# Layer 0's value projection: two chunks of 512 columns with a PSUM bank per token tile, instead of four chunks of 256

## The chip, the core and the metric

The kernel runs on one core of a Trainium2 chip. The metric is the device time of the whole program in microseconds (us). The engines are named as in the profile: PE is TensorE's matmul side and PEld its weight loads, DVE is VectorE, ACT is ScalarE, POOL is GpSimd, SP is the engine whose queue issues most transfers.

## The reference

Two layers over 256 latent tokens and 256 context tokens, width 2048, in float32. Layer 0 projects all 512 tokens with one matrix of 6144 columns and splits the result:

```
qa, ka, va, ga, ub, gb = split(h @ w_in)      # 1024 columns each
ya = neighbourhood_attention(qa, ka, va, ...)  # 8 heads of 128
yb = s5_bidirectional(ub, ...)                 # drive, scan, readout
y  = concat(ya * silu(ga), gelu_glu(yb) * silu(gb)) @ w_out
```

What is changed is the computation of `va`, the values: 512 tokens x 2048 times 2048 x 1024. Layer 1 (grouped-query attention) and the norms are not touched.

## The kernel before, in words

**Matmuls in three parts.** A float32 product is made from two halves of each operand in the faster float32r type. Activations lie in SBUF as `big_h` and `big_l`, 16 k-tiles of 128 x 512 tokens. Each product of a k-tile is three matmuls: high times high, high times low, low times high.

**The weight stream.** `Stream` (lines 338 to 419) carries all weights in one order in pieces of 1024 columns per partition (512 KB). For each piece, `load` issues a transfer on SP into one of four `raw` buffers, `high` makes the `hi` half on ACT (four buffers), `low` subtracts on DVE into `lo` (three buffers). `get` calls `fill`, which issues halves up to three (`lo`) and four (`hi`) pieces on from the piece it then returns, and transfers as `raw` buffers allow:

```
nh, ns = min(self.i + self.n["hi"], n), min(self.i + self.n["lo"], n)   # hi 4, lo 3
```

**The order.** The program's order of instructions on each engine is written out by the trace of this Python code. Work beside the main line stands in generators (`background`); `pump` (line 456), called between groups of matmuls, steps those whose due time by the built-in cost model (`Clock`, line 54) has come, and `force` steps one until a condition holds. Engines then run their queues in that order and wait on semaphores.

**Around the change.** The phase first forms the 16 gate tiles with `aform` (weights stationary, 512 tokens moving, 24 matmuls per piece). Then come the values, `bform4`, called four times (lines 1355 to 1356): a chunk of 256 columns for four token tiles, two token tiles to a bank of the pool `mm`; the activations are stationary and 256 weight columns move. A chunk is four pieces of four k-tiles; for each piece and token tile 12 matmuls are issued and `pump` is called. In the last piece, after the second and the fourth token tile, `done` (`v_out`, line 1345) evacuates a bank: a copy on ACT into `vv0`, a subtraction on DVE into `vv1`, and two transfers of 256 KB to the DRAM tensors `Vd`. The pool `evv` has two buffers of each. After the values the attention heads start; each reads its 128 columns of `Vd` (line 1398).

Beside the values run: `ada_quad` (matmuls into bank `a`, 16 at a time, with 512 KB pieces `aw` loaded as buffers come free), and the S5 generator `s5`: `drive` (uses the three banks of pool `bb`, named `b`), then the scan on DVE, then 16 copies `sx` on ACT written to `Sd`, the table `pe_t` on ACT, and then the 16 output blocks `outp` (line 974): DVE products `ee`, `et`, `di`, matmuls into `sb` banks and one `b` bank `k1` (line 998), copies `kp`, transfers `tt`, matmuls, and the rest.

Of the kernel before, what the change touches and what calls it, by code (L numbers as in the profile page):

```python
# [23 lines left out]
F32 = mybir.dt.float32  # L24
F32R = mybir.dt.float32r
# [5 lines left out]
P = 128  # L31
D = 2048
T = 256
NT = 512
KT = D // P
# [3 lines left out]
EV_IN = 6144  # L39
# [209 lines left out]
def backbone(ctx: ExitStack, tc: tile.TileContext, A, out):  # L249
    nc = tc.nc  # L250
    clock = Clock()
    V, S, PE = Timed(nc.vector, "dve", clock), Timed(nc.scalar, "act", clock), Timed(nc.tensor, "pe", clock)
    GP, SY = Timed(nc.gpsimd, "gp", clock), Timed(nc.sync, "sp", clock)
# [16 lines left out]
    dr = pool(ctx, name="dr", bufs=1, space=bass.MemoryType.DRAM)  # L270
    ctx.enter_context(tc.manual_schedule())

    def bank():
        return bb.tile([P, 512], F32, name="b")
# [17 lines left out]
    def mbank():  # L292
        return mm.tile([P, 512], F32, name="m")
# [7 lines left out]
    big_h = bigp.tile([P, KT, NT], F32R, name="big_h")  # L301
    big_l = bigp.tile([P, KT, NT], F32R, name="big_l")
# [35 lines left out]
    class Stream:  # L338
# [53 lines left out]
                                l[:, :n].rearrange("p (k n) -> p k n", k=nk))  # L392
            self.ns += 1

        def fill(self):

            n = len(self.jobs)
            nh, ns = min(self.i + self.n["hi"], n), min(self.i + self.n["lo"], n)
            while self.nh < nh or self.ns < ns:
                while self.nl < min(self.ns + self.n["raw"], self.i + self.cap, n):  # L400
                    self.load()
                if self.ns < min(ns, self.nh - 1) or self.nh == n:
                    self.low()
                elif self.nh < min(nh, self.nl):
                    self.high()
                else:
                    self.low()
            self.ahead()
# [6 lines left out]
        def get(self):  # L415

            self.fill()
            self.i += 1
            return self.tl.pop(self.i - 1)

    CAP = 4
    ws = Stream()
    W_IN, W_OUT, W_GLU = A["ev_w_in"], A["ev_w_out"], A["s5_glu_w"]
# [9 lines left out]
    def force(b, done=lambda: False):  # L433

        while b in bg and not done():
            clock.floor = b[1]
            step(b)
        clock.floor = 0.0
# [17 lines left out]
    def pump():  # L456
        ws.ahead()
        more = True
        while more:
            more = False  # L460
            for b in list(bg):
                if b[1] <= clock.now():
                    step(b)
                    more = True
# [53 lines left out]
                          stop=(a == 3 and k == 3), skip_group_check=True)  # L518
            pump()

    def bform4(done):

        ps = [mbank().rearrange("p (t n) -> p t n", t=2) for _ in range(2)]
        for a in range(4):
            wh, wl = ws.get()
            for t in range(4):
                c, o = t * P, ps[t // 2][:, t % 2, :]
                for k in range(4):
                    kk = a * 4 + k
                    PE.matmul(o, big_h[:, kk, c:c + P], wh[:, k, :],  # L530
                              start=(a == 0 and k == 0 and t % 2 == 0), stop=False, skip_group_check=True)
                    PE.matmul(o, big_h[:, kk, c:c + P], wl[:, k, :], start=False, stop=False, skip_group_check=True)
                    PE.matmul(o, big_l[:, kk, c:c + P], wh[:, k, :], start=False, stop=(a == 3 and k == 3),
                              skip_group_check=True)
                if a == 3 and t % 2 == 1:
                    done(t // 2, ps[t // 2])
                pump()


    adw = A["ada_w"]  # L540
# [30 lines left out]
    for m in gates:  # L571
        k0 = 2 * NXB if m < NB_ACC - 8 else 0
        ws.add(W_IN, EV_IN, k0, KT - k0, (5 * 1024 if m < 8 else 2 * 1024) + m * P, P)
    for n in range(4):
        for ko in (0, 1):
            ws.add(W_IN, EV_IN, ko * 8, 8, 2 * 1024 + n * 256, 256)
    for h in range(NAH):
        for s in range(2):
            ws.add(W_IN, EV_IN, 0, KT, s * 1024 + h * P, P)
# [21 lines left out]
    Yd = [dr.tile([P, 512], F32, name=f"Yd{m}") for m in range(8)]  # L601
    Bd = [dr.tile([P, 512], F32, name=f"Bd{m}") for m in range(8)]
    Gd = [dr.tile([P, 512], F32, name=f"Gd{m}") for m in range(8)]
    Vd = [dr.tile([P, 2, 4, 256], F32, name=f"Vd{m}") for m in range(4)]
    Sd = [dr.tile([P, 512], F32, name=f"Sd{m}") for m in range(16)]
    Zd = [dr.tile([P, 512], F32, name=f"Zd{m}") for m in range(NAH)]
    Nd = dr.tile([2, P, D], F32, name="Nd")
# [266 lines left out]
    def s5():  # L874
# [60 lines left out]

        yield from several((drive(bt) for bt in range(16)), 6)


        cp = subpool("s5c")
        V.memset(St[:, 0], 0.0)  # L940
# [124 lines left out]
    s5_have = set()  # L1065
# [6 lines left out]
    with ExitStack() as es:  # L1072
# [133 lines left out]
        for b in range(NB):  # L1206
# [11 lines left out]
            for i in range(NB_ACC if b < NXB else 8):  # L1218
                if i % 4 == 0:
                    w = ws.get()  # L1220
# [106 lines left out]
    s5g = background(s5())  # L1327
    for i, m in enumerate(gates):
# [6 lines left out]
        if m < NB_ACC - 8:  # L1335
            part = nxt
            ps = aform(0, NT, KT - 2 * NXB, 2 * NXB)
            V.tensor_add(part, part, ps)
            ps = part
# [3 lines left out]
        SY.dma_start((Bd + Gd)[m], gt)  # L1343

    def v_out(n):
        def done(i, ps):
            vt = [evv.tile([P, NT], F32R, name=f"vv{x}").rearrange("p (t n) -> p t n", t=2) for x in range(2)]
            act(vt[0], ps)
            V.tensor_sub(vt[1], ps, vt[0])
            for x in range(2):  # L1350
                SY.dma_start(Vd[n][:, x, 2 * i:2 * i + 2], vt[x].bitcast(F32))
        return done

    evv = pool(ph1, name="evv", bufs=2, reuse_waits="tile")
    for n in range(4):
        bform4(v_out(n))
    force(adab)
    force(s5g, lambda: "scan" in s5_have)
    ph1.close()
# [31 lines left out]
    def na_head(h, q, k):  # L1391
        (qh, ql), (kh, kl) = q, k
        bias = load_bias(h)
        gl = att.tile([P, NT], F32, name="gl")
        SY.dma_start(gl, Gd[h])
        vh, vl = (att.tile([P, 4, P], F32R, name="v" + x) for x in "hl")
        for x, t in enumerate((vh, vl)):
            SY.dma_start(t.bitcast(F32), Vd[h // 2][:, x, :, (h % 2) * P:(h % 2) * P + P])
        yield
        V.tensor_add(bias.rearrange("p t (k c) -> p t k c", k=4), bias.rearrange("p t (k c) -> p t k c", k=4),  # L1400
                     negm[:, None, None, :].to_broadcast([P, 2, 4, 64]))
        pl = [bank(), bank()]
        for t in range(2):
            c = T + t * P
            mm3(pl[t], qh[:, c:c + P], ql[:, c:c + P], kh, kl, True, True)
        pc = bank().rearrange("p (t k) -> p t k", t=2)
        for t in range(2):
            mm3(pc[:, t], qh[:, t * P:(t + 1) * P], ql[:, t * P:(t + 1) * P], kh[:, :T], kl[:, :T], True, True)
        scored.add(h)
        yield  # L1410
        pr = att.tile([P, 2, NT], F32, name="pr")
        pr2 = att.tile([P, 2, T], F32, name="pr2")
        mx = att.tile([P, 4], F32, name="mx", bufs=2)
        sm = att.tile([P, 4], F32, name="sm", bufs=2)
        for t in range(2):
            act(pr[:, t, :T], pl[t][:, :T], scale=SCALE)
            V.scalar_tensor_tensor(pr[:, t, T:], pl[t][:, T:], SCALE, bias[:, t], op0=OP.mult, op1=OP.add)
        V.tensor_reduce(mx[:, 0:2], pr, axis=AX.X, op=OP.max)
        V.tensor_reduce(mx[:, 2:4], pc, axis=AX.X, op=OP.max)
        V.tensor_scalar(mx[:, 0:2], mx[:, 0:2], -1.0, None, op0=OP.mult)  # L1420
        V.tensor_scalar(mx[:, 2:4], mx[:, 2:4], -SCALE, None, op0=OP.mult)
        yield
        for t in range(2):
            act(pr[:, t], pr[:, t], AF.Exp, bias=mx[:, t:t + 1], accum_out=sm[:, t:t + 1])
        for t in range(2):
            act(pr2[:, t], pc[:, t], AF.Exp, bias=mx[:, 2 + t:3 + t], scale=SCALE, accum_out=sm[:, 2 + t:3 + t])
        V.reciprocal(sm, sm)
        for t in range(2):
            V.tensor_scalar(pr[:, t], pr[:, t], sm[:, t:t + 1], None, op0=OP.mult)
        for t in range(2):  # L1430
            V.tensor_scalar(pr2[:, t], pr2[:, t], sm[:, 2 + t:3 + t], None, op0=OP.mult)
        yield
        def transposed(src):
            p = bank()
            for k_ in range(2):
                for t in range(2):
                    PE.transpose(p[:, k_ * T + t * P:k_ * T + (t + 1) * P], src(t, k_), ident)
            return softmax_pt(p)

        def value(s_, k0, o, start, stop):  # L1440
            for k_ in range(2):
                mm3(o, vh[:, k0 + k_], vl[:, k0 + k_], s_[0][:, k_], s_[1][:, k_],
                    start and k_ == 0, stop and k_ == 1)

        s_ = transposed(lambda t, k_: pr[:, t, k_ * P:(k_ + 1) * P])
        s2 = transposed(lambda t, k_: pr[:, t, (2 + k_) * P:(3 + k_) * P])
        po = bank()
        yield
        value(s_, 0, po[:, T:], True, False)
        s3 = transposed(lambda t, k_: pr2[:, t, k_ * P:(k_ + 1) * P])  # L1450
        value(s2, 2, po[:, T:], False, True)
        yield
        value(s3, 0, po[:, :T], True, True)
        z = att.tile([P, NT], F32, name="zo")
        V.tensor_mul(z, po, gl)
        if h == NAH - 1:
            zl.append(z)
        else:
            SY.dma_start(Zd[h], z)
        yield  # L1460
# [499 lines left out]
```

## Time and profile before

| | us |
|---|---|
| median of 3 runs | 1521.24 (1519.86 to 1521.37) |
| the profiled execution | 1517.6 |
| its span, first to last instruction | 1515.7 |
| PE busy in the span | 1472.3 (97%) |
| DVE busy | 958.2 (63%) |
| ACT busy | 645.8 (43%) |
| mean granted TensorE clock | 0.989 |

Busy PE time counts pipelined matmuls at their full length, so neighbouring ones overlap; the time that a matmul takes out of PE is its distance to the next. The chain of waits is followed back from the last instruction, at each step to what released it.

### The profile page before, as it was taken

The page shows a single profiled execution, that of the slowest core. Times are in us where ns is not written, and L with a number is a line of the kernel's source. Part 1 is how long each engine was busy: PE and PEld are TensorE (multiplying, and loading weights), DVE is VectorE, ACT ScalarE, POOL GpSimd, SP SyncE. Part 2 cuts the span into 40 slices and gives each one's busy share as a digit, 9 for nine tenths or more (in the row PEclk, how much of TensorE's full clock was granted, in tenths as well). Part 3 has the DMA queues.
Part 4 walks back from the last instruction along what each step waited for, and adds up shares of the span by engine and source line. Part 5 has one row for each costly group of instructions (what it writes and reads, how often), then busy time and mean ns, then how long its engine had stood idle before and what let it go on. Part 6 is the DMA issues. An engine that isn't in the chain of part 4 may idle for free.

```text
span 1515.7 us, 30530 instructions
## 1 busy us (share of the span) xinstructions
PE 1472.3 (97%) x12530; PEld 1281.6 (85%) x12530; DVE 958.2 (63%) x1721; ACT 645.8 (43%) x981; POOL 153.7 (10%) x308
## 2 busy tenths in 40 slices
PE   6999999999999999999999999999999999999995
PEld 3676877777789977888788999999999999999995
DVE  5356468788422888544447765755765766677587
ACT  2333345422455434433345433433454555656540
POOL 1000000000000032300000000100511211121021
PEclk8999999999999999999999999999999999999998
DMA  9999376776897676677776698885566454445684
GB/s 326 337 333 291 111 219 211 227 244 215 264 292 251 176 198 150 162 236 232 216 243 222 234 351 288 272 303 181 173 205 181 128 158 132 140 120 151 211 252 143
DMA packets 329920, 332.70 MB, mean 220 GB/s; under 512 B 40197, under 2 KB 287925, under 8 KB 329141
## 3 DMA queue, kind: packets, MB, share of 16 engines
q1 hardware_dynamic: 323540, 314.87, 66.5%
q0 software_dynamic: 6240, 15.88, 3.9%
q8 instruction: 98, 1.61, 0.4%
q14 instruction: 42, 0.34, 0.1%
HBM read 301.92 MB, written 24.54 MB: 215 GB/s over the span
## 4 chain that ended last, share of the span: by engine, by line
PE 83%; DMA 5%; DVE 4%; issue 4%; POOL 2%; ACT 1%; SPq 1%; DVEq 0%; POOLq 0%; ACTq 0%
PE m L212 61%; PE b L212 12%; PE a L212 6%; PE sb L212 4%; DMA raw<-in_ev_w_in_dram 1%; DVE t L212 1%; SPq L212 1%; DMA aw<-in_ada_w_dram 1%; DMA gf<-in_ln_b_dram 1%; DMA nat<-in_s_c_im_dram 1%; POOL gbr L212 1%; POOL rt L212 1%; DVE lo L212 1%; DMA tt<-kp 0%; POOL xp L212 0%
## 5 line engine op out<-in xcount | busy, mean ns | idle before, releaser
L212 ACT ACTIVATE hi<-raw 128x1024 fp32r<-128x1024 f32 (+1 forms) x253 | 265.2, 1050 | 306.9 <-PE m L212 164.2
L212 PE MATMUL m<-hi,big_h 128*128 128x256 f32 x1224 | 351.3, 287 | 0.2 <-DVE t L212 0.2
L212 PE MATMUL m<-hi,big_l 128*128 128x256 f32 x1224 | 347.1, 284 | 0.0
L212 DVE TENSOR_TENSOR lo<-raw,hi 128x1024 fp32r<-128x1024 f32 (+1 forms) x214 | 257.3, 1209 | 112.5 <-issue 54.5
L212 PE MATMUL m<-lo,big_h 128*128 128x256 f32 x1152 | 326.5, 283 | 0.0
L212 PE MATMUL m<-big_h,hi 128*128 128x512 f32 (+1 forms) x848 | 319.1, 376 | 1.9 <-DVE acc L212 1.2
L212 PE MATMUL m<-big_l,hi 128*128 128x512 f32 (+1 forms) x848 | 309.1, 364 | 0.0
L212 PE MATMUL m<-big_h,lo 128*128 128x512 f32 (+1 forms) x832 | 304.4, 366 | 0.0
L212 PEld LDWEIGHTS m<-hi,big_h 128*128 128x128 f32 x1224 | 235.2, 192 | 7.4 <-issue 6.7
L212 PEld LDWEIGHTS m<-hi,big_l 128*128 128x128 f32 x1224 | 235.3, 192 | 0.2 <-DVE big_l L212 0.2
L212 PEld LDWEIGHTS m<-lo,big_h 128*128 128x128 f32 x1152 | 221.5, 192 | 0.1
L212 PEld LDWEIGHTS m<-big_h,hi 128*128 128x128 f32 x848 | 159.9, 189 | 39.6 <-issue 11.3
L212 PEld LDWEIGHTS m<-big_h,lo 128*128 128x128 f32 x832 | 157.0, 189 | 26.4
L212 PEld LDWEIGHTS m<-big_l,hi 128*128 128x128 f32 x848 | 160.2, 189 | 21.1
L212 PE MATMUL m<-lox,big_h 128*128 128x256 f32 x384 | 108.6, 283 | 0.0
L212 PE MATMUL m<-hix,big_h 128*128 128x256 f32 x312 | 89.1, 285 | 0.0
L212 PE MATMUL m<-hix,big_l 128*128 128x256 f32 x312 | 88.3, 283 | 0.0
L212 POOL DMA_DIRECT2D Yd<-ys x64 | 37.7, 595 | 395.8 <-DVE ys L212 395.1
L212 PEld LDWEIGHTS m<-lox,big_h 128*128 128x128 f32 x384 | 73.6, 192 | 0.3
L212 ACT ACTIVATE hix<-raw 128x1024 fp32r<-128x1024 f32 x45 | 47.5, 1056 | 53.3 <-DMA raw<-in_od_w_out_dram 17.9
L212 PE MATMUL a<-aw,cst 128*32 128x256 f32 x1024 | 64.8, 383 | 1.2 <-DMA aw<-in_ada_w_dram 1.2
L212 DVE TENSOR_TENSOR lox<-raw,hi 128x1024 fp32r<-128x1024 f32 x39 | 47.6, 1222 | 22.3 <-PE m L212 15.7
(383 smaller groups left out, 2167.9 us busy)
## 6 DMA issues: line engine op xcount, KB each, us to landing
aw<-in_ada_w_dram SPq DMA_DIRECT2D x128, 512.0 KB, 5.8
raw<-in_od_w_in_dram SPq DMA_DIRECT2D x96, 512.0 KB, 3.8
raw<-in_ev_w_in_dram SPq DMA_DIRECT2D x90, 512.0 KB, 4.9
adp<-in_ada_w_dram SPq DMA_DIRECT2D x64, 512.0 KB, 7.9
raw<-in_ev_w_out_dram SPq DMA_DIRECT2D x64, 512.0 KB, 5.0
raw<-in_od_w_out_dram SPq DMA_DIRECT2D x32, 512.0 KB, 4.3
ub<-Ud SPq DMA_DIRECT2D x32, 128.0 KB, 4.9
Sd<-sx SPq DMA_DIRECT2D x16, 256.0 KB, 6.1
```

The lines of the kernel that those rows point to most:

```text
L212: r = f(*a, **kw)
```

## The change

The values are formed in two chunks of 512 columns. A chunk has 8 pieces of two k-tiles and 512 columns each (rows of 2 KB in DRAM instead of 1 KB). Four banks are taken per chunk, one for each token tile: both of `mm` and two of the three of `bb`; before the first chunk the S5 generator is stepped until its `drive` part is through. Pieces are taken in pairs (`get2`). For each pair and token tile, 12 matmuls of 512 columns are issued in two parts of 6, each followed by `pump`. In the last pair `done` follows each token tile. `Vd` becomes two tensors. Matmuls of this part: 768 of 256 columns before, 384 of 512 after.

```diff
-        def fill(self):
+        def fill(self, m=99):
-            nh, ns = min(self.i + self.n["hi"], n), min(self.i + self.n["lo"], n)
+            nh, ns = min(self.i + min(m, self.n["hi"]), n), min(self.i + min(m, self.n["lo"]), n)
...
+        def get2(self, fill=True):
+            if fill or self.ns < min(self.i + 2, len(self.jobs)):
+                self.fill()
+            self.i += 2
+            return self.tl.pop(self.i - 2), self.tl.pop(self.i - 1)
...
-    def bform4(done):
...
+    def wpart(ps, w, c, korder, a):
+        wh, wl = w
+        for k in range(2):
+            kk = korder[a * 2 + k]
+            PE.matmul(ps, big_h[:, kk, c:c + P], wh[:, k, :], start=a == 0 and k == 0, stop=False)
+            PE.matmul(ps, big_h[:, kk, c:c + P], wl[:, k, :], start=False, stop=False)
+            PE.matmul(ps, big_l[:, kk, c:c + P], wh[:, k, :], start=False, stop=a == 7 and k == 1)
+        pump()
+
+    def wide4(done, korder, ps):
+        for a in range(4):
+            w = ws.get2(a < 3)
+            for t in range(4):
+                for j in range(2):
+                    wpart(ps[t], w[j], t * P, korder, 2 * a + j)
+                if a == 3:
+                    done(t, ps[t])
+                    if t == 0:
+                        ws.fill(1)
...
-    for n in range(4):
-        for ko in (0, 1):
-            ws.add(W_IN, EV_IN, ko * 8, 8, 2 * 1024 + n * 256, 256)
+    for n in range(2):
+        ws.add(W_IN, EV_IN, 0, KT, 2 * 1024 + n * 512, 512)
...
-    Vd = [dr.tile([P, 2, 4, 256], F32, name=f"Vd{m}") for m in range(4)]
+    Vd = [dr.tile([P, 2, 4, 512], F32, name=f"Vd{m}") for m in range(2)]
...
         yield from several((drive(bt) for bt in range(16)), 6)
+        s5_have.add("drive")
...
-        def done(i, ps):
-            vt = [evv.tile([P, NT], F32R, name=f"vv{x}").rearrange("p (t n) -> p t n", t=2) for x in range(2)]
+        def done(t, ps):
+            vt = [evv.tile([P, 512], F32R, name=f"vv{x}") for x in range(2)]
             act(vt[0], ps)
             V.tensor_sub(vt[1], ps, vt[0])
             for x in range(2):
-                SY.dma_start(Vd[n][:, x, 2 * i:2 * i + 2], vt[x].bitcast(F32))
+                SY.dma_start(Vd[n][:, x, t], vt[x].bitcast(F32))
...
-    for n in range(4):
-        bform4(v_out(n))
+    force(s5g, lambda: "drive" in s5_have)
+    for n in range(2):
+        wide4(v_out(n), tuple(range(KT)), [mbank(), mbank(), bank(), bank()])
...
-            SY.dma_start(t.bitcast(F32), Vd[h // 2][:, x, :, (h % 2) * P:(h % 2) * P + P])
+            SY.dma_start(t.bitcast(F32), Vd[h // 4][:, x, :, (h % 4) * P:(h % 4) * P + P])
```

## Rows read from the trace of the kernel before

**Rows 1.** The page's chain of waits: shares of the span by line.
```profile
PE m L212 61%; PE b L212 12%; PE a L212 6%; PE sb L212 4%; DMA raw<-in_ev_w_in_dram 1%; DVE t L212 1%; SPq L212 1%; DMA aw<-in_ada_w_dram 1%; DMA gf<-in_ln_b_dram 1%; DMA nat<-in_s_c_im_dram 1%; POOL gbr L212 1%; POOL rt L212 1%; DVE lo L212 1%; DMA tt<-kp 0%; POOL xp L212 0%
```

**Rows 2.** Busy time by stretch: from:to, length, PE, PEld, DVE, ACT, POOL, clock, DMA.
```profile
412.00:441.00 29.00, 29.00 (x267) 26.05 (x266) 6.22 (x7) 15.07 (x20) 0.00 (x0) 1.00 0.88 284
495.00:528.00 33.00, 32.14 (x569) 30.25 (x569) 27.68 (x46) 13.78 (x28) 2.39 (x4) 1.00 0.56 163
```

**Rows 3.** Instructions on tile m, 395 to 545: count, duration min/median/max, first and last start.
```profile
L212 PE MATMUL m<-hi,big_h x256: 278/283/386, 412.4 to 527.4; 128*128 128x256 f32 x128
```

**Rows 4.** Chain of waits in order of time, 412 to 500: start, length, what.
```profile
460.94 5.94 PE m L212 x48
466.88 1.00 PE a L212 x16
467.88 8.82 PE m L212 x72
```

**Rows 5.** The same chain, 300 to 400, in the gates.
```profile
309.37 5.71 PE m L212 x24
...
316.07 7.75 PE m L212 x33
```

**Rows 6.** The same chain, 500 to 545, between S5's output blocks.
```profile
509.76 0.50 PE sb L212 x24
...
511.89 4.50 PE m L212 x36
...
517.00 1.62 PE m L212 x12
...
533.16 1.59 PE m L212 x6
```

**Rows 7.** Timeline of DVE: start, length, instruction, idle before and releaser.
```profile
440.97 0.69 DVE L212 TENSOR_TENSOR vv<-m,vv 128x512 fp32r<-128x512 f32 x1 [3.37 <-ACT vv L212]
...
473.80 1.23 DVE L212 TENSOR_TENSOR lo<-raw,hi 128x1024 fp32r<-128x1024 f32 x1 [4.43 <-issue]
...
506.38 1.21 DVE L212 TENSOR_TENSOR lo<-raw,hi 128x1024 fp32r<-128x1024 f32 x1
...
509.64 1.21 DVE L212 TENSOR_TENSOR lo<-raw,hi 128x1024 fp32r<-128x1024 f32 x1
```

**Rows 8.** Timeline of SP's queue, 435.5 to 443.
```profile
436.90 1.05 SPq L212 DMA_DIRECT2D Vd<-vv  x2
```

**Rows 9.** Timeline of ACT, 434 to 519.
```profile
436.28 0.60 ACT L212 ACTIVATE vv<-m 128x512 fp32r<-128x512 f32 x1 [1.82 <-PE m L212]
...
505.45 1.06 ACT L212 ACTIVATE hi<-raw 128x1024 fp32r<-128x1024 f32 x1 [3.47 <-PE m L212]
507.86 0.27 ACT L212 ACTIVATE kp<-b 128x112 f32<-128x112 f32 x1 [1.35 <-PE b L212]
```

**Rows 10.** Transfers on tile Vd, 430 to 470, first two chunks: issue to landing.
```profile
DMA to landing us min/median/max: 5.9/6.5/7.3
```

**Rows 11.** Transfers on tile Vd, 485 to 540, last two chunks: issue to landing.
```profile
DMA to landing us min/median/max: 2.4/2.4/2.4
```

**Rows 12.** Who waited for whom on PE, 500 to 530: total, times, longest.
```profile
PE sb L212 <- DVE di L212: 0.9, 1, 0.9
```

**Rows 13.** Instructions on tile dT: the matmuls of drive, first and last start.
```profile
L212 PE MATMUL b<-ub,dT x512: 222/222/369, 212.6 to 299.2; 128*64 128x64 f32 x171
```

**Rows 14.** Timeline of PE, 506 to 511 and 574 to 586.
```profile
510.19 0.30 PE L212 MATMUL b<-ee,bbar 64*32 64x112 f32 x4
...
580.43 1.34 PE L212 MATMUL sb<-sx,ee 128*64 128x64 f32 x32 [3.55 <-DMA sx<-Sd]
```

**Rows 15.** DMA issues, 425 to 432: count, KB each, median us to landing.
```profile
aw<-in_ada_w_dram SPq DMA_DIRECT2D x3, 512.0 KB, 6.7
```

**Rows 16.** DMA queues, 440 to 450: packets, MB, share of 16 engines.
```profile
q1 hardware_dynamic: 1565, 3.16, 97.2%
```

**Rows 17.** Busy time by stretch, columns as in rows 2.
```profile
580.00:585.00 5.00, 4.57 (x42) 3.88 (x43) 3.91 (x7) 0.89 (x3) 2.35 (x4) 0.66 0.91 204
```

## Prediction before the run

> **What bounds the kernel now.** I read the chain of waits first: it is to be seen there that matmuls of TensorE (PE) into four kinds of banks carry 61 + 12 + 6 + 4 = 83% of the span, those into the `m` banks most, and no single kind of transfer over 1% [rows 1]. So a change counts by the PE time that it takes out or puts in. Then the stretches of the values' stage: PE is busy 29.00 of 29.00 us in its first quarter and 32.14 of 33 in its last; VectorE (DVE) has 6 us of work in the first and 28 in the last, where the S5 output blocks run [rows 2]. Then the groups by shape: the stage's 768 matmuls are three groups of 256, each 128x256, from 412.4 us on (one of the three stands there) [rows 3]. Their 283 ns are the length of one in the pipeline, not its share of the time; the distance from one to the next comes from the chain, where only the number of matmuls differs between two steps: (8.82 - 5.94) / 24 = 0.120 us [rows 4].
>
> **The matmuls.** 768 of 256 columns go, 384 of 512 come; the stationary operand is the same 128x128 token block, so half as many weight loads go with them. The stage of before has no 512-wide matmul; the gates ahead of it have, with split weights and `big_h`/`big_l` in exchanged roles: (7.75 - 5.71) / 9 = 0.2267 us from one to the next [rows 5]. 768 x 0.120 = 92.2 us against 384 x 0.2267 = 87.1: -5.1 us. From the other side: 512 columns at twice 0.120 would save nothing. I take the row, since width and clock (1.00, which is 2.4 GHz) are the same and only the source of the moving columns differs.
> Against the columns alone at that clock (107 and 213 ns) both distances are 13 ns longer: a fixed part per matmul, and 384 times it is the 5.1 us.
> The Trainium skill (TensorE: Matmul & The Clock Gate, section Back-to-back issue gap) gives the isolated gap as N/2.4 + 2.5 ns, so a fixed part of only 2.5, and by it the exchange would be worth 83.9 - 82.9 = 1.0 us; the rows, at 13, disagree with it.
>
> **Entering and leaving.** A run of value matmuls between two other groups takes more than its count: 48 take 5.94 us, 0.18 over 48 x 0.120 [rows 4]; 24 wide ones 5.71, 0.27 over 24 x 0.2267 [rows 5]. Ten ada groups of 16 lie inside the stage (one row of the ten stands there [rows 4]) and stay, so 10 x 0.09 = 0.9 us comes back. Around S5's blocks it is 1.62 for 12 (0.18 over) against 1.59 for 6 (0.23 over) [rows 6]; some eight such edges give 0.4. Together +1.3 us. Bounds: 0.4 (the ada edges alike after all) and 2.
>
> **The split of the weights.** Now two pieces are used per step. There are three `lo` buffers, and `get2` leaves pieces split up to one beyond the pair, so at each call the second piece of the coming pair has no `lo` yet. Its buffer is that of the last pair's first piece, which PE reads until six matmuls (1.36 us) before the pair ends. The subtraction takes 1.21 to 1.23 us [rows 7], and PE asks for its result seven matmuls (1.59 us) after the pair's start. Where DVE has nothing else, 1.36 + 1.59 covers 1.23 and it costs nothing; this holds for five of the seven steps from one pair to the next. Before, each `lo` was made two pieces (11.5 us) ahead. `get2(False)` in the last pair does not hold back: seven pieces are split where eight are wanted, so it fills as always, and `fill(1)` then finds nothing to do but loads.
>
> **The step from the first chunk to the second.** Here the cover is gone. The four evacuations now follow each other at 12 matmuls, 2.72 us, where before two stood 2.9 us apart and then 24 us passed. Each takes one `vv0` and one `vv1` of which there are two, so the third and fourth evacuation wait for the `Vd` transfers of the first and second. With S the start of the chunk's last pair: the second token tile ends at S + 5.44; its activation starts 0.2 later and takes 0.6, its first transfer is issued at S + 6.25 (436.90 for an activation at 436.28) [rows 8, 9], the other 0.8 later after the subtraction. In this stretch a `Vd` transfer lands 5.9 to 7.3 us after issue, median 6.5 [rows 10]: so S + 13.55 until both buffers are free, then the fourth subtraction (0.69) [rows 7] and behind it on DVE the `lo` of the second piece (1.23): S + 15.5. PE wants it at S + 10.88 + 1.59 = S + 12.5. A wait of 3.0 us; in general landing time less 3.5. Behind the waiting activation on ScalarE (ACT) stand the next pair's two `hi` (2.1 us, wanted 10.9 us later) and S5's `sx` copies, behind DVE's wait only the two `lo`. Bounds: 1.2 us where the transfers land at 2.4 as in the late evacuations [rows 11], since the subtraction and the `lo` still come one after the other; 3.8 at 7.3. I take 3.0, the median of this stretch. At the second chunk's end the transfers land at 2.4 us and the buffers are free in time: nothing.
>
> **The last pair.** At its start S5's blocks fill DVE. In the trace PE releases ACT's `hi` of that boundary at 505.45 [rows 9], but its `lo` runs at 509.64, 4.2 us late, behind S5's work and behind the `lo` of the boundary before it, which ran at 506.38 [rows 7]. One of these two falls away: 3.0 us late, done 4.2 after the boundary. PE wants it at 1.6 plus the S5 block that stands in between, 2.1 us (509.76 to 511.89) [rows 6]. That is 0.5 us. Bounds: -0.9, if the wait of 0.9 us for `di` [rows 12] goes with the earlier start; +2.9, if none of the lag is taken up and no block stands in between (5.4 - 1.6 = 3.8, less the 0.9).
>
> **At nothing.** The two banks from S5's pool: `drive` ended at 299.2 us [rows 13], so the `force` runs nothing. For the second chunk S5's output blocks have one bank for `k1` instead of three; the copy out of it starts at 507.86 and takes 0.27, the next block writes at 510.19 [rows 9, 14], 2 us to spare; without that cover some 0.6 us a block, four blocks. `Vd` keeps its 16 writes of 256 KB, the weights 16 loads of 512 KB on SP, in longer rows; the reads per head keep 512-byte rows. The ada pieces land 6.7 us after issue [rows 15], and groups come every 5.94 + 1.00 us now, 6.71 then: PE did not wait for them [rows 2], so nothing; if it were tight all through, 10 x 0.23 = 2.3 us are lost.
>
> **Sum.** -5.1 + 1.3 + 3.0 + 0.5 = -0.3 us: a span of 1515.4 and an execution of 1517.3 against the profiled 1517.6 (1515.7 and 1.9 around it). That execution is 3.6 us below the median of the runs; on the median, 1521.24 - 0.3 = 1520.9 us. What remains after the stage is bound by PE again, so a gain or loss there carries to the end.
>
> **Rivals.** About 0.2%, 3.0 us, is what a measurement tells from no change.
> Faster: the waits stay at their lower bounds, since the transfers land early and DVE is ahead of PE in the last pair. Then -5.1 + 1.3 + 1.2 - 0.9 = -3.5: 1517.7 us. For it: DVE idles through most of the first three quarters, and late transfers land at 2.4 us [rows 11]. Against: the third and fourth evacuation fall into the loaded stretch.
> Slower: the boundary wait grows until the clock falls. Eight `Vd` transfers (2.1 MB) now come within 9 us on queues that are at 97.2% of their share with four [rows 16]. A PE wait of 3.55 us in this trace (up to 580.43) was followed by a granted clock of 0.66, between its two levels of 1.2 and 2.4 GHz, over 5 us [rows 14, 17]: 1.7 us lost. At a landing time of 9 us the wait is 5.5, with the clock 7.2 instead of 3.0: 1520.9 + 4.2 = 1525.1 us. It decides the sign from a landing time of 8.1 us on (4.6 + 1.7 = 6.3, a sum of +3.0). Against: the first two evacuations, whose landing counts, are no denser than before.
> No saving in the matmuls: if 512 columns from the weight buffers take twice what 256 take (0.240), the sum is 1.3 + 3.0 + 0.5 = +4.8 and the time 1526.0 us. The rows of the gates speak against it [rows 5].
> By the skill's formula above the sum would be +3.8 and the time 1525.0; it goes with this rival's chance.
>
> **How the numbers follow.** Forecast 0.43, faster rival 0.28, slower rival 0.22, no saving 0.07. With the boundary wait between 1.2 and 3.8 us and the last pair's between -0.9 and 1.5 the forecast's own range is 1518 to 1523; the range goes on to the rivals, 1516.6 to 1525.8. Faster by over 0.2% (below 1518.2): most of the faster rival and the low edge of the forecast, 0.27; slower (above 1524.3): the last two and a little of the forecast, 0.28; within: 0.45.
>
> **What would show it.** The distance of the wide value matmuls (0.227). One gap on PE of 2 to 4 us, six to seven matmuls into the second chunk, put down to `lo` on DVE, and the third and fourth `vv` activation waiting for `Vd`. A wait of 0 to 2 us in the last pair. The ada groups entered and left 0.09 us dearer. It is wrong if PE shows no gap at the boundary, or if the wide distance is 0.24.

## The result, and the profile after

The changed kernel takes 1530.47 us (median, 1523.52 to 1537.86) against 1519.47 for the kernel before (1516.66 to 1521.37): ratio 1.0063 with a 95% interval of [1.0048, 1.0078]. The medians are 11.0 us apart, and the new one lies outside the predicted range of 1516.6 to 1525.8. The profiled execution took 1529.65 us, its span is 1527.9 at a clock of 0.987.

The loss is read best by cutting both spans at the same instructions. Ahead of the values every engine has the same instructions in the same order, so the time of any of them can be compared. The row is that of the drive inputs written to `Ud`; the last two numbers are the starts of the first and last issue. Before, then after:

```profile
L212 SPq DMA_DIRECT2D Ud<-up x8: 319/328/348, 187.8 to 194.1; - x8
```
```profile
L212 SPq DMA_DIRECT2D Ud<-up x8: 319/328/350, 194.2 to 200.5; - x8
```

6.4 us are lost before anything that was changed has run. What PE waited for in the second half of that time, from 90 us to 188 in before and to 194 in after (total us, times, longest):

```profile
PE m L212 <- DVE acc L212: 1.2, 1, 1.2
PE sb L212 <- DMA nat<-in_s_c_im_dram: 0.9, 1, 0.9
```
```profile
PE sb L212 <- DMA nat<-in_s_c_im_dram: 2.2, 1, 2.2
PE sb L212 <- DMA nat<-in_s_b_im_dram: 1.8, 1, 1.8
PE m L212 <- DVE acc L212: 1.4, 1, 1.4
```

`nat` is the buffer into which S5's weights `s_b_re`, `s_b_im`, `s_c_re` and `s_c_im` are loaded, 512 KB each. PE waited 4.0 us for two of these loads, against 0.9 before, and behind these waits the clock cost 3.4 us (it was at 1.2 GHz for 3.4 us from 99.3 and again from 157.3), against nothing before. The 3.1 us more of waiting and the 3.4 of clock are the early loss.

The first value matmul comes at 412.4 before [rows 3] and at 419.0 after. The second cut is the last pair of splits of the attention output in layer 0, on DVE, before and after:

```profile
861.00 1.29 DVE L212 SCALAR_TENSOR_TENSOR big_l<-za,big_h 128x512 fp32r<-128x512 f32 x2
```
```profile
870.42 1.29 DVE L212 SCALAR_TENSOR_TENSOR big_l<-za,big_h 128x512 fp32r<-128x512 f32 x2
```

From the first value matmul to this cut, "the middle" below, it is 448.6 us before and 451.4 after; from there to the end, "the rest", 654.7 and 657.4. So the 12.2 us between the two spans are, to within rounding, 6.6 early, 2.8 in the middle, 2.7 in the rest. What the change was priced for lies in the middle alone.

Who waited on PE there (total us, times, longest), 412 to 861 before, then 419 to 870 after:

```profile
PE sb L212 <- DMA sx<-Sd: 3.6, 1, 3.6
PE sb L212 <- DVE di L212: 0.9, 1, 0.9
PE a L212 <- ACT aw L212: 0.7, 1, 0.7
```
```profile
PE m L212 <- DVE lo L212: 3.8, 2, 2.3
PE sb L212 <- DMA tt<-kp: 2.8, 3, 2.0
PE sb L212 <- DVE di L212: 2.3, 1, 2.3
PE a L212 <- DMA aw<-in_ada_w_dram: 0.9, 1, 0.9
```

5.2 us of waits have become 10. The two for `lo`, 3.8 us, are the predicted ones; those for S5 (`tt`, `di`, `sx`) changed places, 4.5 before and 5.1 after. The chain of waits in order of time shows the wide matmuls and the step between the chunks (start, length, what):

```profile
437.77 1.00 PE a L212 x16
438.77 1.60 PE m L212 x6
440.38 4.10 PE b L212 x18
444.48 1.00 PE a L212 x16
...
467.86 7.33 DMA Vd<-vv
476.54 1.23 DVE lo L212
477.81 5.74 PE m L212 x17
```

24 wide matmuls between two ada groups take 1.60 + 4.10, 5.71 us from 438.77 to 444.48, to the hundredth what 24 took in the gates [rows 5]. The stretches of [rows 2] again, 6.6 us later (columns as there):

```profile
419.00:448.00 29.00, 28.06 (x166) 20.14 (x165) 6.55 (x6) 14.84 (x18) 0.00 (x0) 1.00 0.79 252
502.00:535.00 33.00, 29.21 (x466) 22.76 (x465) 25.81 (x43) 14.73 (x27) 2.40 (x4) 1.00 0.57 156
```

PE falls from 32.14 to 29.21 us in the second. In the rest, waits for ada weights (before at 950 to 1060, after at 957 to 1070):

```profile
PE a L212 <- DMA aw<-in_ada_w_dram: 0.9, 1, 0.9
```
```profile
PE a L212 <- DMA aw<-in_ada_w_dram: 3.0, 1, 3.0
```

### The profile page after: what moved, and what is told of

Its sections match the earlier page's. It is cut to its first block, busy times and chain, and to the rows that moved or that the text cites. A ratio compares the mean times of both kernels' runs of the same rounds, so it can differ in the third digit from the quotient of the medians.

```text
span 1527.9 us, 29770 instructions
## 1 busy us (share of the span) xinstructions
PE 1473.9 (96%) x12146; PEld 1262.3 (83%) x12146; DVE 958.4 (63%) x1721; ACT 645.1 (42%) x981; POOL 154.1 (10%) x308
## 4 chain that ended last, share of the span: by engine, by line
PE 80%; DMA 7%; DVE 4%; issue 4%; POOL 2%; ACT 1%; SPq 1%; DVEq 0%; ACTq 0%; POOLq 0%
PE m L212 58%; PE b L212 13%; PE a L212 6%; PE sb L212 4%; DMA raw<-in_ev_w_in_dram 2%; DMA aw<-in_ada_w_dram 1%; DVE t L212 1%; DMA nat<-in_s_b_im_dram 1%; DMA nat<-in_s_c_im_dram 1%; DMA gf<-in_ln_b_dram 1%; SPq L212 1%; POOL gbr L212 1%; DMA tt<-kp 1%; POOL rt L212 1%; DVE lo L212 1%
## 5 line engine op out<-in xcount | busy, mean ns | idle before, releaser
L212 PE MATMUL m<-hi,big_h 128*128 128x256 f32 (+1 forms) x1032 | 304.5, 295 | 0.7 <-DVE t L212 0.7
L212 PE MATMUL m<-hi,big_l 128*128 128x256 f32 (+1 forms) x1032 | 300.8, 292 | 0.0
L212 PE MATMUL m<-lo,big_h 128*128 128x256 f32 (+1 forms) x960 | 280.3, 292 | 3.8 <-DVE lo L212 3.8
L212 PEld LDWEIGHTS m<-hi,big_h 128*128 128x128 f32 x1032 | 199.2, 193 | 7.8 <-issue 4.7
L212 PEld LDWEIGHTS m<-hi,big_l 128*128 128x128 f32 x1032 | 199.0, 193 | 3.0 <-DVE big_l L212 0.2
L212 PEld LDWEIGHTS m<-lo,big_h 128*128 128x128 f32 x960 | 185.4, 193 | 7.0 <-DVE lo L212 4.5
L212 PEld LDWEIGHTS m<-hix,big_h 128*128 128x128 f32 x312 | 59.8, 192 | 0.9 <-issue 0.4
```

What stands on the lines that cost most here:

```text
L212: r = f(*a, **kw)
```

## The experiments

The table has, of each profile, the start of the first `Ud` issue, the middle with PE's idle time and the time lost to the lower clock in it (half of the time at 1.2 GHz), and the rest (of the padded kernels without the padding). The median stands beside that of before on the same chip; e7 and e8 are one execution each.

| kernel | Ud | middle | idle | clock | rest | median / before |
|---|---|---|---|---|---|---|
| before | 187.8 | 448.6 | 5.2 | 1.7 | 654.7 | 1519.47 |
| after | 194.2 | 451.4 | 10.2 | 1.7 | 657.4 | 1530.47 / 1519.47 |
| e1 before again | 187.4 | 448.5 | 5.0 | 1.7 | 652.7 | 1520.9 / 1520.82 |
| e2 after again | 193.0 | 454.4 | 11.0 | 5.1 | 656.7 | 1531.0 / 1520.82 |
| e3 after, ring of 4 | 190.2 | 454.0 | 9.6 | 6.8 | 657.7 | 1526.87 / 1520.82 |
| e4 before, new Vd | 187.9 | 448.4 | 4.9 | 1.7 | 654.6 | 1520.86 / 1520.82 |
| e5 single, ring of 4 | 192.4 | 460.2 | 12.0 | 6.8 | 657.6 | 1530.8 / 1521.62 |
| e6 single, ring of 2 | 187.9 | 457.4 | 11.5 | 8.5 | 657.9 | 1532.6 / 1521.62 |
| e7 after, padded | 188.1 | 455.6 | 10.4 | 6.8 | 657.2 | 1538.68 / 1521.62 |
| e8 before, padded | 188.6 | 450.5 | 5.9 | 3.4 | 655.2 | 1532.84 / 1521.62 |
| e9 e6, ada 1.0 us apart | 194.5 | 445.3 | 5.5 | 0.0 | 657.8 | 1523.37 / 1521.37 |
| e10 before, ada 1.0 us apart | 190.8 | 448.3 | 4.3 | 1.7 | 659.3 | 1519.95 / 1521.37 |
| e11 as e7 | 192.3 | 453.8 | 8.4 | 6.8 | 661.1 | 1538.71 / 1521.37 |
| e12 as e8 | 187.9 | 449.5 | 5.6 | 1.7 | 655.5 | 1531.42 / 1521.37 |
| e13 before, S5 loads in 1 KB | 190.1 | 448.6 | 5.1 | 1.7 | 655.6 | 1521.01 / 1522.22 |
| e14 after, S5 loads in 1 KB | 190.1 | 451.7 | 8.6 | 3.4 | 657.9 | 1527.48 / 1522.22 |
| e15 before, S5 loads on POOL | 188.3 | 445.7 | 3.0 | 0.0 | 658.5 | 1524.85 / 1522.22 |
| e16 after, S5 loads on POOL | 188.4 | 457.4 | 14.0 | 6.8 | 658.0 | 1535.57 / 1522.22 |
| e17 e9, ada matmuls later | 193.3 | 448.8 | 6.5 | 3.4 | 653.9 | 1521.29 / 1522.78 |
| e18 e10, ada matmuls later | 187.9 | 448.9 | 5.3 | 1.7 | 653.5 | 1521.83 / 1522.78 |

**e1 and e2, both kernels again.**

> The kernel before, once more, for a second profile. In the first one the values' stage began at 412.4 us; in the changed kernel's it began at 419.0, although the program's order of instructions on every engine is the same up to there. Theory A (the first 412 us differ from one execution to the next): this run may begin its values anywhere from 411 to 420 us, and the time is within 0.2% of before (ratio 0.998 to 1.002). Theory B (the early part depends on the kernel, by where its DRAM tensors lie): the values begin at 412 to 413 us again.

> The changed kernel once more. Theory A: its values may begin anywhere from 411 to 420 us; the stage and what follows it together are again 5 to 6 us longer than before, ratio 1.003 to 1.006. Theory B: the values begin at 418 us or later, ratio 1.005 to 1.008. Both: a wait of PE of 1.2 to 4 us for lo near the start of the second chunk.

Before: ratio 0.9998 [0.9982, 1.0013]. After: 1.0065 [1.005, 1.0079]. The loss is there again, the early 5 to 6 us among it: the values begin at 411.9 and at 418.2 us. That is theory B's forecast, but later profiles don't keep to it: the changed values begin at 411.9 and 413.4 in e6 and e7, the old ones at 415.6 in e10.

**e3, evacuation buffers 4 deep.**

```diff
-    evv = pool(ph1, name="evv", bufs=2, reuse_waits="tile")
+    evv = pool(ph1, name="evv", bufs=4, reuse_waits="tile")
```

> The changed kernel with four buffers of vv0 and vv1 instead of two, so that no evacuation waits for a Vd transfer. If that ring is what delays the split at the step from the first chunk to the second: PE's wait for lo there falls from 2.3 us to 1.2 or less, the drop of the clock behind it (0.94 over 468 to 495 us) goes, S5's table pe_t comes some 3 us earlier after the start of the values, and the run is 3 to 6 us faster than the changed kernel. If instead the pairs as such (one lo too few) cost the time, the wait stays above 2 us and the time within 2 us of the changed kernel.

1.0037 [1.0023, 1.005]. Waits on PE in its middle:

```profile
PE sb L212 <- DVE di L212: 4.9, 1, 4.9
PE sb L212 <- DMA tt<-kp: 3.8, 5, 1.5
PE a L212 <- ACT aw L212: 0.7, 1, 0.7
```

No wait for `lo` is left: with the pairs, a ring of two makes them, as predicted. But 4.9 us of waiting turn up at S5's first output block instead, the clock costs 6.8 us in place of 5.1, and the middle is as long as in e2. The median is 4.1 us under e2's, as forecast, but not for the reason forecast: in the profile 2.8 us of the gain stand at the early mark.

**e4, before with the changed `Vd` alone** (two tensors of 512 columns).

> The kernel before with only its DRAM tensors for the values laid out as in the changed kernel (two of 512 columns instead of four of 256; the order of the work is the same). Theory A: no change, ratio 0.998 to 1.002. Theory B: slower by 4 to 7 us, with the loss before 200 us.

1.0008 [0.9996, 1.0021], nothing early and nothing in the middle: the tensor's layout alone does not cost the time.

**e5 and e6, one piece at a time.**

```diff
-        for a in range(4):
-            w = ws.get2(a < 3)
+        for a in range(8):
+            w = ws.get()
             for t in range(4):
-                for j in range(2):
-                    wpart(ps[t], w[j], t * P, korder, 2 * a + j)
-                if a == 3:
+                wpart(ps[t], w, t * P, korder, a)
+                if a == 7:
                     done(t, ps[t])
-                    if t == 0:
-                        ws.fill(1)
```

> After, but the 512-column weights are split and used one piece at a time (eight pieces a chunk, as before) and evacuation buffers are 4 deep. In the two profiles of after, the stretch from the first value matmul to the end of layer 0 (the last split of the attention output) is 451.4 and 454.4 us long against 448.6 before, and PE sits idle in it for 10.2 and 11.0 us against 5.2. Theory A (the pairs and the short ring make the weights late): no wait for lo in 410-560, idle back to 5 to 6 us, that stretch 443 to 446 us, the median 1521 to 1524 us with the early loss still there. Theory C (S5's output blocks are paced by VectorE, and shorter matmuls cover less of it): the lo waits go, PE waits for di and tt instead, idle stays at 9 to 11 us, the stretch 451 to 454 us, the median 1526 to 1530 us. Early loss (Ud issued at 190 to 194 against 187.8): either size, A and C say nothing of it.

> After with one piece at a time and evacuation buffers still 2 deep, so that the pairs alone are undone. Theory A: the ring alone keeps one lo wait of 2 to 3 us at the chunk boundary, idle 7 to 8 us, the stretch from the first value matmul to the end of layer 0 446 to 449 us, median 1523 to 1526 us. Theory C: as after, idle 9 to 11 us, 451 to 454 us, median 1527 to 1531 us.

1.006 [1.0036, 1.0084] and 1.008 [1.0052, 1.0108]: both medians and both middles lie above what either theory gave, theory A's by far. The waits fit neither. In e6's middle they are

```profile
PE a L212 <- DMA aw<-in_ada_w_dram: 6.9, 8, 4.1
PE sb L212 <- DMA tt<-kp: 2.1, 4, 0.9
PE sb L212 <- DVE di L212: 1.8, 2, 1.1
PE a L212 <- ACT aw L212: 0.7, 1, 0.7
```

No `lo` even with two buffers, and less for S5 than before had. All of the added idle time is a new wait, some 250 us behind the values, for ada weights: S5 finishes later by the planner's clock, the ada loads beside the heads start a head later, and their last two groups are forced together ahead of the last head (e5 has 4.1 us of it, in seven waits). The stretch has the clock at 0.66 of its full 2.4 GHz on the mean:

```profile
775.00:800.00 25.00, 17.38 (x139) 8.87 (x132) 6.38 (x15) 5.17 (x7) 0.00 (x0) 0.66 0.70 231
```

**e9 and e10, that pile taken away; and before with the same number.**

```diff
-            adab = background(ada_quad(1, 1, 1024, ap3, 8, 8, 2.0))
+            adab = background(ada_quad(1, 1, 1024, ap3, 8, 8, 1.0))
```

> e6 (one piece at a time, evacuation buffers 2 deep) with one number changed: the 32 loads of ada weights that run beside the heads of layer 0 are asked for 1.0 us apart instead of 2.0. In e6 PE waited 6.7 us for aw at 778 to 793 and its clock was at 1.2 GHz for 17.1 us there (8.5 us lost), because the last two groups of ada matmuls were left over for the last head. Theory D (what e5 and e6 lost is this pile alone; the values in single pieces are a gain): waits for aw under 1.5 us, no fall of the clock at 780 to 800, the stretch from the first value matmul to the end of layer 0 442 to 445 us against 457.4 in e6 and 448.6 in before, the median 1513 to 1519 us by where the early part falls. Theory C (S5's blocks cost the time in any layout): the pile goes, and 4 us and more come back as waits for di and tt: 448 to 452 us, median 1520 to 1525 us.

> Control for e9: before with the same one number (ada loads 1.0 us apart). Before has no such pile (one wait of 0.72 us for aw at 786), so the median stays at 1520 to 1522 us; if it falls by over 2 us, the gain of e9 is not the values'.

e9: 1.0009 [0.9989, 1.0028]; e10: 0.9993 [0.9978, 1.0009]. The same stretch of e9 has PE at 23.54 us and the clock at 1.00:

```profile
775.00:800.00 25.00, 23.54 (x166) 18.35 (x165) 14.60 (x26) 12.35 (x22) 0.00 (x0) 1.00 0.80 242
```

The pile is gone, as theory D has it, and the middle is 445.3, 3.3 under before and just above D's 442 to 445. PE's waits for S5's blocks are 3.7 us against 4.5 in before, so C's waits did not come. But the median, 1523.37, misses D's 1513 to 1519 and lies in C's range: by the time alone nothing is gained, since this profile lost 6 us early and 3 in the rest. Of theory A this is left: the waits for `lo` need both the pairs and the ring of two, for e3, with a deeper ring, and e6, without the pairs, have none. What the pairs cost with the two numbers of e9 and e17 was not run.

**e17 and e18, the wait in the rest; and before with the same two numbers.**

```diff
-            clock.ready = when[n0 + g - 1] + 1.0
+            clock.ready = when[n0 + g - 1] + (3.0 if (l, s) == (1, 2) else 1.0)
```

> e9 with a second number changed: the ada matmuls beside layer 0's output projection are put 3.0 us behind the planned landing of their weights, not 1.0. In e9 one of them held PE for 2.88 us at 991.7 and the clock was at 1.2 GHz for 3.4 us behind it (1.7 us lost). If that wait is what the late part costs: no wait for aw over 0.9 us at 950 to 1060, the stretch from the end of layer 0 to the end 653 to 655 us against 657.8 in e9 and 652.7 to 654.7 in before, the median 2 to 5 us under e9's, 1516 to 1521 us, 0.1 to 0.4 per cent under before. If the late part has another cause, it stays at 657 to 658 us and the median at e9's 1.001 of before.

> Control: before with the same two numbers. Before waits for aw 0.88 us at 988, so there is at most 1 us to gain: 1518 to 1521 us. What e17 has under this is the values'.

e17: 0.999 [0.9972, 1.0008], e18: 0.9996 [0.9976, 1.0016]. All waits on PE of e17 at 950 to 1065:

```profile
PE b L212 <- DVE t L212: 0.3, 1, 0.3
```

The wait for `aw` is gone and the rest is 653.9 against 657.8 in e9, as forecast: that wait, and the clock behind it, made e9's late loss. The wait isn't the values' own: in e10, before with one number changed, the planner puts the group early as well, PE waits 1.8 us for it, and the rest is 659.3, which the wait explains only in part. e17 takes back the 10 us of after, but its median, 1521.29, just misses the forecast of 1516 to 1521, and it isn't told from before, nor from e18. Its middle is 448.8, as long as e18's 448.9 and 3.5 us longer than e9's; one wait for `aw` is 1.2 longer there (1.95 us at 789.3) and the clock takes 3.4. So the shorter middle stands in one profile of two.

**e7, e8, e11, e12, the early loss: padding at the end.** 384 tiny matmuls behind the last one that counts give after as many matmuls as before has.

```diff
                 SY.dma_start(dram(out, i * P * D + c * 512, [[D, P], [1, 512]]), parts[c][0])
+        pad = mbank()[:32, :32]
+        for i in range(384):
+            PE.matmul(pad, ident[:, :32], ident[:, :32], start=True, stop=True)
```

> After with 384 tiny matmuls (32x32, results unused) at the very end, behind the last matmul that counts: the program is as long as before's again, and all that runs before 1500 us is as it was in after. Only the early part is read: Ud issued at 187.4 to 187.9 in three profiles of before and its like, at 194.2 and 193.0 in two of after. Theory P (where the loaded program and its data lie decides how fast the 512 KB S5 loads run): Ud comes back to 187 to 189 us, or at least moves by over 2 us. Rival Q (something in the changed instructions themselves, or chance from run to run): 192 to 195 us under the first half of it, anything under the second.

> Before with the same 384 tiny matmuls at the very end. Theory P: the early part may move (Ud later than 189 us) though nothing that runs ahead of it is changed; if it stays at 187 to 188, P is not refuted, since not every length need be a bad one. Q: 187 to 188 us.

> e7 again (after, 384 tiny matmuls at the end), timed. The tail costs 10.7 us in the profile of e7 and 10.6 in that of e8. Theory P: the early loss of after (6.4 and 5.2 us in two profiles) stays away, so that this median less that of e12 is 4 to 6 us, where after less before was 11.0 and 10.2. Q by chance from run to run: 10 to 11 us.

> e8 again (before, the same tail), timed: 1531 to 1532 us, 10 to 11 above before, by both.

The early loss was absent in e7 and back in e11, the same kernel. The padded medians, e11's and e12's, differ by 7.3 us, between the 4 to 6 of theory P and the 10 to 11 of chance. The length of the program is not shown to matter.

**e13 to e16, the S5 loads.** Why these loads come late can be seen in part in three stretches, before and then after.

```profile
60.00:70.00 10.00, 10.00 (x68) 6.72 (x68) 5.28 (x8) 2.99 (x5) 0.00 (x0) 1.00 1.09 282
70.00:80.00 10.00, 10.00 (x72) 6.61 (x71) 5.28 (x13) 2.78 (x4) 0.00 (x0) 1.00 1.08 365
90.00:100.00 10.00, 10.00 (x72) 6.90 (x71) 5.18 (x8) 1.72 (x3) 0.00 (x0) 1.00 1.08 268
```
```profile
60.00:70.00 10.00, 10.00 (x68) 6.72 (x68) 5.31 (x8) 2.99 (x5) 0.00 (x0) 1.00 1.10 247
70.00:80.00 10.00, 10.00 (x72) 6.62 (x71) 5.25 (x13) 1.60 (x3) 0.00 (x0) 1.00 1.08 365
90.00:100.00 10.00, 8.23 (x60) 5.14 (x58) 4.31 (x6) 0.45 (x2) 0.00 (x0) 0.96 1.09 214
```

The DMA engines are equally busy (1.08 to 1.10) in all, yet move 365 GB/s in the middle one and far less in the other two, and after less than before. The first follows the issue of S5's `s_b_re` at 57.92, the last that of `s_b_im` at 82.8 (84.0 in after): both 512 KB.

```diff
-            SY.dma_start(t.rearrange("g (k n) -> g k n", k=2),
-                         dram(A[nm], 0, [[1024, G], [G * 1024, 2], [1, 1024]]))
+            for q in range(4):
+                SY.dma_start(t.rearrange("g (k n) -> g k n", k=2)[:, :, q * 256:q * 256 + 256],
+                             dram(A[nm], q * 256, [[1024, G], [G * 1024, 2], [1, 256]]))
```

That is e13 and e14; e15 and e16 leave the load whole and move it:

```diff
-            SY.dma_start(t.rearrange("g (k n) -> g k n", k=2),
+            GP.dma_start(t.rearrange("g (k n) -> g k n", k=2),
```

> Before, with each of S5's four 512 KB loads (s_b_re, s_b_im, s_c_re, s_c_im) cut into four of 128 KB with packets of 1 KB. Theory N (these loads' 4 KB packets make the early stretches slow, more or less so by chance): Ud issued at 185 to 188, GB/s in 60:70 and 90:100 above the 281 and 268 of before, median 1518 to 1521 us. Rival (it is not their packets): as before, 187 to 191 and 1520 to 1522 us.

> After with the same. Theory N: Ud at 185 to 189, and the median only 4 to 7 us above that of e13 (what the values stage and the later wait for aw cost: 2.8 to 7 and 2.5 us in the profiles, less what varies), where after is 10 above before. Rival: Ud at 190 to 195 and 9 to 11 us above e13.

> Before with S5's four loads on GpSimd's queue, beside the others and not in line with them. The planner then also places some ada groups and S5 steps otherwise. Theory N: no stretch of 60 to 160 us under 280 GB/s at a full DMA share, the early part as long as in before or shorter. Rival: as slow as before or slower.

> After with the same. Theory N: the marks up to the first value matmul are those of e15 within 1 us, and the median is 4 to 7 us above e15. Rival: 3 to 6 us later than e15 already at the first value matmul, and 9 to 11 us above.

In 1 KB packets the stretches are as slow as before (276 and 268 GB/s in e13, 272 and 261 in e14), so the size of these loads' packets is not it. On POOL's queue the rate falls too, only elsewhere. In e16 the two loads are issued here:

```profile
L212 POOL DMA_DIRECT2D nat<-in_s_b_re_dram x1: 648/648/648, 4.1 to 4.1; - x1
L212 POOL DMA_DIRECT2D nat<-in_s_b_im_dram x1: 586/586/586, 82.8 to 82.8; - x1
```

The first is 54 us earlier than on SP, so 60 to 70 us, at 357 GB/s, has no such load in it. The second lies at the old time, and the fall comes at 85 to 90 us (in before it is deepest at 90 to 95, with 191 GB/s):

```profile
60.00:70.00 10.00, 10.00 (x73) 7.12 (x72) 3.90 (x6) 2.99 (x5) 0.00 (x0) 1.00 1.09 357
85.00:90.00 5.00, 5.00 (x39) 3.58 (x38) 1.23 (x3) 1.78 (x4) 0.00 (x0) 1.00 1.08 220
90.00:100.00 10.00, 10.00 (x69) 6.90 (x67) 6.63 (x9) 2.45 (x4) 0.00 (x0) 1.00 1.09 356
```

In e15 it is 233 GB/s there. So theory N's stretches without a fall did not come, and the place in SP's queue is not shown to be the cause. In e15 and e16 PE waits for none of these loads, and both reach `Ud` at 188.3 and 188.4; but the first value matmul follows at 415.3 and at 418.0, 2.7 us apart where theory N allowed 1, and the medians are 10.7 apart, as far as with the loads on SP. Moving the loads did not take the difference away. (The planner also places ada groups otherwise in the two, and e16's middle has 14.0 us idle, 7.3 of it one wait for `di`.)

What is shown of the early loss is that PE waits for S5's loads and loses clock behind the waits. With these loads on SP, `Ud` is reached at 187.4 to 190.8 with the old values, six of eight below 189, and at 187.9 to 194.5 with the new, two of ten below 189. The two overlap, and why a later change should move them stays open. Where the early marks agree, e13 and e14, the change costs 5.5 us in the profiles, 3.1 in the middle and 2.3 in the rest; the medians, which hold executions with other early marks too, are 6.5 apart.

## Why the prediction was wrong

**Right.** The matmuls: 0.227 us apart at the median, and 24 of them between two ada groups in 5.71. With the edges they were to give 3.8 us; the middle less idle and clock loss is 441.7 us before and 439.5, 438.3, 438.4 and 438.6 in after, e2, e7 and e11, so 2.2 to 3.4 were got. By the isolated gap of the Trainium skill (TensorE: Matmul & The Clock Gate, section Back-to-back issue gap) it would have been 1.0 ahead of the edges; the distance measured speaks against that here too. The boundary: one wait, at the seventh matmul of the second chunk, 2.3 us for 3.0 predicted. The chain is the one named, a full ring, then `lo`, but only the fourth activation waited for a `Vd` transfer; the two transfers of the first evacuation landed 4.9 and 4.6 us after issue, in time for the third:

```profile
469.98 0.60 ACT L212 ACTIVATE vv<-b 128x512 fp32r<-128x512 f32 x1 [2.15 <-PE b L212]
475.30 0.60 ACT L212 ACTIVATE vv<-b 128x512 fp32r<-128x512 f32 x1 [4.72 <-DMA Vd<-vv]
```

The last pair: 1.4 us for 0.5, inside its bounds. `drive` had long ended, and the new `Vd` costs nothing (e4).

**Wrong.** The step that failed is the last of the sum, "What remains after the stage is bound by PE again, so a gain or loss there carries to the end", together with the ada groups, which it put "at nothing" beside the values and did not follow further. The sum of -0.3 us came out as +4.7 in the middle, and two more losses lie where the sum has no term:
- In the middle the waits grew by 4.7 us (mean idle of after, e2, e7, e11 10.0; of before, e1, e4, e8, e12 5.3) where 3.5 was forecast, and the clock took 3.1 more (5.1 against 2.0) where only the slower rival had it. The matmuls with their edges gave 3.1 of the 3.8. Together that is +4.7 for a forecast of -0.3. The clock's part is the slower rival's mechanism; but it fell after waits of 1.4 to 3.5 us at several places, not after one of 5.5 at the boundary.
- In the rest the planner's order has the ada groups 12 matmuls earlier among those of layer 0's output projection, and one of them waits 3.0 us for its weights instead of 0.9. In the first two profiles the rest is 2.7 us longer, on the mean of the nine 3.6; in e17, with that group put later, the wait and the loss are gone.
- The early part, 4.1 us on the mean of the same profiles (first value matmul at 416.9 against 412.8) and 6.6 in the first, lies ahead of the change. A sum that starts where the code changes can't hold it. It is time that PE waits for S5's loads, and clock lost behind that; why these loads come later under the changed program stays open.

The matmuls' gain stands apart from the waits: less idle and clock loss the middle is 439.8 us in e9 and 438.9 in e17, against 442.2 and 441.9 in e10 and e18, before with the same numbers. As whole time it was never got. e9's middle is 3.3 us shorter than before's, but e17's is not, e15 has one of 445.7 with the old values, and no kernel with wide values is told to be faster than before by its median.

## What to carry to other kernels

Where a planner writes out the order, a change of one stage shifts every due time behind it, so look for background work that is held to a deadline later on (here ada groups 250 and 450 us on) before a saved microsecond is carried to the end. Cut both traces at instructions that come in the same order in both, and price only the pieces: here one loss in three lay before the change. When an experiment that removes a wait doesn't move the time, read where its waits went before the theory is dropped; e6 looked like a failure of its theory, and one number took away the pile of waits that hid what it had removed. And before a fall in a rate is called gone, look at where the transfer now lies: on POOL's queue it had only moved out of the stretches that were compared.

## What was not expected of the hardware

Behind the issue of one of S5's 512 KB loads the rate of the 16 DMA engines falls at a full busy share: in 10 us from 365 to between 214 and 282 GB/s. It falls with the load cut to 1 KB packets as well (261 to 276), and with the load on POOL's queue (220 and 233 over 5 us). How long PE then waits varies between executions of one kernel: for `s_c_im` it is 1.1 us in e7 and 2.8 in e11, which reach `Ud` 4.2 us apart. What makes the rate fall is not shown. These loads fill 64 of the 128 partitions, where the pieces of weights beside them fill all; no run changed that.

A PE wait of 2.35 us in after, up to 477.8, was followed by the clock at 1.2 GHz for 3.4 us from 478.1; another of 2.34 us, up to 516.1, was not, and in e7 one of 1.39 us, up to 555.5, was. So the length of the wait alone does not tell here. After's two stretches:

```profile
478.00:483.00 5.00, 5.00 (x16) 3.93 (x16) 0.89 (x1) 4.44 (x6) 0.00 (x0) 0.66 0.78 229
516.00:521.00 5.00, 4.90 (x179) 4.16 (x180) 4.83 (x10) 1.39 (x5) 0.00 (x0) 1.00 0.16 24
```
